# One stock of 19 tile buffers for loads and outputs, and later stores, in a chunked RWKV-WKV kernel

## The chip, the cores and the metric

The kernel runs on one core of a Trainium2 chip. TensorE (PE) multiplies matrices into PSUM, VectorE (DVE) and ScalarE (ACT) do elementwise work, GpSimd (POOL) does small work, and SyncE (SP) only issues transfers between HBM and SBUF. The transfers are carried by 16 DMA engines. The metric is the device time of one execution in microseconds (us). Profile times are counted from the start of the span, which runs from the first to the last instruction.

## The reference

The inputs are `k` and `v` of shape (16, 2048, 256) in float32 (batch, time, channel), and `w` and `u` with one number for each channel. For every batch and channel there is a recurrence over time with a numerator state `aa`, a denominator state `bb` and a running maximum `pp` that keeps the exponentials in range:

```python
ww = u + kk; qq = np.maximum(pp, ww)
e1, e2 = np.exp(pp - qq), np.exp(ww - qq)
output[b, t, :] = (e1 * aa + e2 * vv) / (e1 * bb + e2 + 1e-08)
ww = pp - w + kk; qq = np.maximum(ww, kk)      # qq becomes the next pp
e1, e2 = np.exp(ww - qq), np.exp(kk - qq)
aa = e1 * aa + e2 * vv
bb = e1 * bb + e2
```

So an output is a ratio of two decayed sums over all earlier steps, in which the current step counts with the bonus `u`. Without intermediate results, 67.1 MB are read and 33.5 MB are written.

## The kernel before

**Tiles.** Time is cut into 16 chunks of 128 steps, and a chunk into four tiles of four batches each, so there are NP = 64 tiles. Tile n belongs to chunk n // 4. It has its 128 steps on the partitions and 4 x 256 = 1024 columns (batch, channel). Each tile needs one load of `k`, one load of `v` and one store, each of 512 KB and each one DMA. That makes 191 large DMAs, and four of 128 KB for the last tile.

**The work of one tile.** `round_k` (DVE, L176) copies the loaded keys to a type that PE takes, and with that the load's buffer is free again. `logs` (PE) adds decay terms to the keys in PSUM, and `exps` (ACT, L204) takes the exponential of both variants (without and with the bonus) into the ring `EZR` of 12 tiles. `cast_v` (DVE, L209) copies the loaded values to bf16, which frees the other buffer, and `times_v` (DVE, L214) multiplies. `den` (PE) sums the denominators over time. `den_log` (ACT, L346) takes their logarithm out of PSUM into a buffer `RD[n]`, and `den_exp` (ACT, L349) turns it there into the reciprocal. `num` (PE, L358) sums the numerators, and `mult` (DVE, L362), in two halves, multiplies them into the same buffer. `store` (SP, L365) sends that buffer to HBM. Between chunks, small steps (`sums`, `turn`, `state_...`, `turn_back`, `inject`) carry the state on. They need several slots, which is why outputs run LAG = 10 tiles behind the exponentials.

**Slots.** The order on every engine is the order in which the program text emits the instructions. Slot n is one pass of a loop: `exps(n)`, then the rounding of the keys of tile n+2, the casting of values, `times_v(n)` and `logs(n+1)`. From slot 10 on it also has `den` and the reciprocal of tile n-10, and the two `mult`s of tile n-11. In a slot, ACT has `exps(n)`, then `den_log(n-10)`, then `den_exp(n-10)`. After slot 63 a tail works off the remaining outputs, of which ACT's two exponentials of the very last tile are done by halves.

**Transfers.** All loads and stores are issued by SP from one queue, in program order. In `before` they have three pools of fixed size: six buffers for keys, five for values, and eight for outputs. At the start of slot n, `load(n + AHEAD)` emits the loads of the values of tile n+5 and the keys of tile n+6. Then `store(qp - 2)` follows, which is the output of tile n-13:

```python
load(n + AHEAD)
if qp >= 2:            # qp = n - 11
    store(qp - 2)
```

A load waits on SP until the buffer that it takes has been rounded or cast. `den_log` of tile q takes the output buffer of tile q-8, and waits on ACT until that tile's store has landed. A transfer also waits for the eighth transfer before it, whose semaphore it takes over.

Of the kernel before, what the change touches and what calls it, by code (L numbers as in the profile page):

```python
# [7 lines left out]
F32 = mybir.dt.float32  # L8
# [7 lines left out]
def kernel(  # L16
# [9 lines left out]
    K = tc.keep_in_program_order  # L26
    PE, DVE, SC, POOL, SP = nc.tensor, nc.vector, nc.scalar, nc.gpsimd, nc.sync

    B, T, Dm = k.shape
# [3 lines left out]
    D = 2 * Dm  # L33
    NP = 4 * NST
    RING = 12
    AHEAD = 6
    LAG = 10
    RS = 2.0 ** -20
    CAP = 54.0
    ON_DVE = (0, 1, NST - 1)  # L40

    consts = ctx.enter_context(tc.tile_pool(name="consts", bufs=1))
    kpool = ctx.enter_context(tc.tile_pool(name="kpool", bufs=AHEAD))
    vpool = ctx.enter_context(tc.tile_pool(name="vpool", bufs=5))
    vbpool = ctx.enter_context(tc.tile_pool(name="vbpool", bufs=4))
    rpool = ctx.enter_context(tc.tile_pool(name="rpool", bufs=8))
    small = ctx.enter_context(tc.tile_pool(name="small", bufs=2))
    tiny = ctx.enter_context(tc.tile_pool(name="tiny", bufs=1))
    ps = ctx.enter_context(tc.tile_pool(name="ps", bufs=1, space=bass.MemoryType.PSUM))
# [2 lines left out]
    kr_of, vr_of, VB = {}, {}, {}  # L52

    def rows_of(x, n):
        c, p = divmod(n, 4)
        return x[4 * p:4 * p + 4, c * TC:(c + 1) * TC, :].rearrange("n t d -> t n d")

    def load_k(n, queue=SP):
        kr_of[n] = kpool.tile([128, 4, Dm], F32, tag="kr", name="kr")
        K(queue.dma_start(out=kr_of[n], in_=rows_of(k, n)))  # L60

    def load_v(n, queue=SP):
        vr_of[n] = vpool.tile([128, 4, Dm], F32, tag="vr", name="vr")
        K(queue.dma_start(out=vr_of[n], in_=rows_of(v, n)))


    def load(n):
        if n - 1 < NP:
            load_v(n - 1)
        if n < NP:  # L70
            load_k(n)

    def matrix(name, dt):
        return consts.tile([128, 128], dt, tag=name, name=name)

    def fill(ap, value):
        K(DVE.memset(ap.bitcast(F32) if ap.dtype == F32R else ap, value))
# [27 lines left out]
    load_k(1)  # L107
    load_row(SP, 1, 2, u)
    load_v(0)
    for n in range(2, AHEAD):  # L110
        load_k(n)
        load_v(n - 1)
    K(SC.preload_act_table_set("natural_log_exp_and_others"))
# [34 lines left out]
    def out_matrices(*names):  # L148
        if "L" in names:
            for h in range(2):  # L150
                fill(Lx[HS * h:HS * h + HS, HS * (1 - h):HS * (2 - h)], 0.0)
        for name in names:
            x, f = I1 if name[0] == "I" else Lx, RS if name[-1] == "N" else 1.0
            mats[name] = matrix(name, BF16)
            K(DVE.tensor_single_scalar(mats[name], x, f, op=ALU.mult))
# [15 lines left out]
    def ez(n):  # L171
        return EZR[:, :, n % RING]

    def round_k(n):
        km = consts.tile([128, 4, Dm], F32R, tag=f"km{n % 2}", name="km") if n < 2 else KM[n - 2]
        K(DVE.tensor_copy(km, kr_of.pop(n)))  # L176
        KM[n] = km

    def logs(n):
        km = KM[n].rearrange("p (i n) d -> p i (n d)", i=2)  # L180

        def rows(q):
            for i in range(2):
                g = 32 * (2 * q + i)
                K(PE.matmul(half(n, q)[:, i, :], CO[g:g + 32, :],  # L185
                            WU[g:g + 32, :].unsqueeze(1).broadcast_to([32, 2, Dm]), start=True, stop=False,
                            tile_position=(g, 0), skip_group_check=True))

        def steps(q):
            for i in range(2):  # L190
                K(PE.matmul(half(n, q)[:, i, :], (NLE, NLZ)[q], km[:, i, :], start=False, stop=True,  # L191
                            skip_group_check=True))

        rows(0)
        rows(1)
        steps(0)
        steps(1)

    def exps(n):
        if n < TURNS:  # L200
            for q in range(2):
                K(SC.activation(ez(n)[:, q], half(n, q), ACT.Exp))  # L202
        else:
            K(SC.activation(ez(n)[:, 0:2], PS[:, 0:4, :].rearrange("p (q i) x -> p q i x", q=2), ACT.Exp))  # L204

    def cast_v(n):
        vb = vbpool.tile([128, 4, Dm], BF16, tag="vb", name="vb")
        vr = vr_of.pop(n)
        K(DVE.tensor_copy(vb, vr))  # L209
        VB[n] = vb  # L210

    def times_v(n):
        vb = VB.pop(n).rearrange("p (i n) d -> p i (n d)", i=2)
        K(DVE.tensor_mul(ez(n)[:, 2:4], ez(n)[:, 0:2], vb.unsqueeze(1).broadcast_to([128, 2, 2, D])))  # L214
# [16 lines left out]
    def sums(n):  # L231
        c, p = divmod(n, 4)
        t = MISC[:, 0:Dm]
        for o in range(2):
            x = 24 - 16 * o - 2 * p
            for j in range(4):
                q, i = divmod(j, 2)
                K(PE.matmul(t[32 * j:32 * j + 32, :], mats["OH"][:, x:x + 32],  # L238
                            ez(n)[:, 2 * q, i, Dm * o:Dm * o + Dm],
                            start=p == 0 and o == 0, stop=p == 3 and o == 1,  # L240
                            tile_position=(0, 32 * j), skip_group_check=True))
# [94 lines left out]
    RD = {}  # L336
# [5 lines left out]
                            skip_group_check=True))  # L342

    def den_log(n, bank=DENB):
        RD[n] = rpool.tile([128, 2, D], F32, tag="rd", name="rd")
        K(SC.activation(RD[n], bank, ACT.Ln, scale=RS))  # L346

    def den_exp(n, i=slice(0, 2)):
        K(SC.activation(RD[n][:, i, :], RD[n][:, i, :], ACT.Exp, scale=-1.0))  # L349
# [10 lines left out]
    def mult(n, bank, i):  # L360
        rd = RD[n]
        K(DVE.tensor_mul(rd[:, i, :], bank, rd[:, i, :]))  # L362

    def store(n):
        K(SP.dma_start(out=rows_of(out, n), in_=RD.pop(n).rearrange("p i (n d) -> p (i n) d", n=2)))  # L365

    later = {}
    for c in range(NST):
# [19 lines left out]
    def small_work(n, where):  # L388
        for f, c in later.pop((n, where), []):
            f(c)  # L390

    def idle_matmuls(n, bank):
        for _ in range(n):
            K(PE.matmul(bank, idle[:, 0:128], idle, start=True, stop=True, skip_group_check=True))
# [5 lines left out]
    K(DVE.scalar_tensor_tensor(WU, WUH, Rest, wuf, ALU.mult, ALU.add))  # L400
    logs(0)
    round_k(1)
    cast_v(0)
    for n in range(LAG):

        load(n + AHEAD)
        exps(n)
        if n % 4 == 0 and n:
            sums(n - 1)
        small_work(n, "act")  # L410
        small_work(n, "logs")
        logs(n + 1)
        if n % 4:
            sums(n - 1)
        small_work(n, "pe")
        idle_matmuls(2, NUMB)
        times_v(n)
        small_work(n, "chain")
        round_k(n + 2)
        small_work(n, "round")  # L420
        cast_v(n + 1)
        if n < 4:
            (state_start, lambda: out_matrices("L"), lambda: out_matrices("IdN", "LN"),
             lambda: out_matrices("Id"))[n]()

    def inverses(n):
        q, qp = n - LAG, n - LAG - 1
        if qp >= 0:
            num(qp, NUMB, 1)

        sums(n - 1)
        if n + 1 < NP:
            recip(q, lambda: small_work(n, "recip"))

    for n in range(LAG, NP):

        q, qp = n - LAG, n - LAG - 1
        load(n + AHEAD)

        if qp >= 2:  # L440
            store(qp - 2)
        if qp >= 0:
            num(qp, NUMB, 0)
        den(q)
        small_work(n, "nums")
        exps(n)
        small_work(n, "act")
        if qp >= 0:
            mult(qp, NUMB, 0)
        small_work(n, "mid")  # L450
        if n == LAG:

            inverses(n)
            small_work(n, "early")
        if n + 2 < NP:
            round_k(n + 2)

        if n % 4 in (3, 0):
            cast_v(n)
        if n + 1 == NP:  # L460
            times_v(n)
        elif n % 4 < 2:
            cast_v(n + 1)
        if n > LAG:
            inverses(n)
        if qp >= 0:
            mult(qp, NUMB, 1)
        small_work(n, "scan")
        if n + 1 < NP:
            times_v(n)  # L470
            small_work(n, "chain")
            logs(n + 1)
        small_work(n, "pe")
# [4 lines left out]
    q, c = NP - LAG - 1, NST - 1  # L478
# [4 lines left out]
    def outputs(n):  # L483
        for i in range(2):
            mult(n, nbank(n, i), i)
        store(n)

    den_log(q)
    den(q + 1, dbank(q + 1))
    sums(NP - 1)  # L490
    copy_sums(c)
    store(q - 2)
    store(q - 1)
    den_exp(q)
    den_log(q + 1, dbank(q + 1))
    tile_num(q, 0)
# [9 lines left out]
    state_offsets(c)  # L506
    state_weights(c)
    mult(q, nbank(q, 1), 1)
    store(q)
    state_chain(c)  # L510
    den(q + 3, dbank(q + 3))
    for i in range(2):
# [14 lines left out]
    n, p = NP - 1, (NP - 1) % 4  # L527
    for i in range(2):
        den_exp(n, slice(i, i + 1))
        mult(n, nbank(n, i), i)  # L530
        for j, eng in ((0, SP), (1, SC)):
            b = 4 * p + 2 * i + j
            K(eng.dma_start(out=out[b, c * TC:(c + 1) * TC, :], in_=RD[n][:, i, Dm * j:Dm * j + Dm]))
# [31 lines left out]
```

## Time and profile before

| what | value |
|---|---|
| time, median of 3 runs (lowest to highest) | 290.09 us (289.56 to 290.15) |
| the profiled execution | 289.65 us, with a span of 288.0 us |
| mean granted TensorE clock | 0.988 |
| busy share of the span: PE, DVE, ACT, POOL | 91%, 91%, 88%, 37% |
| bytes moved, mean rate | 101.54 MB, 353 GB/s |
| issue to landing, median: keys, values, outputs | 8.3, 8.3, 8.1 us |

Engines wait for each other through semaphores. "Busy" is the time in which an engine executes, and an SP row is the time that SP needs to issue a transfer, not the time of the transfer itself. A busy share over the whole span is a mean over stages: an engine with 91% can be full in one stage and starved in another, so the stages have to be looked at one by one. The DMA share is the mean busy share of the 16 DMA engines, and in full stages it shows a little over 1.

### The profile page before, as it was taken

The page shows a single profiled execution, that of the slowest core. Times are in us where ns is not written, and L with a number is a line of the kernel's source. Part 1 is how long each engine was busy: PE and PEld are TensorE (multiplying, and loading weights), DVE is VectorE, ACT ScalarE, POOL GpSimd, SP SyncE. Part 2 cuts the span into 40 slices and gives each one's busy share as a digit, 9 for nine tenths or more (in the row PEclk, how much of TensorE's full clock was granted, in tenths as well). Part 3 has the DMA queues.
Part 4 walks back from the last instruction along what each step waited for, and adds up shares of the span by engine and source line. Part 5 has one row for each costly group of instructions (what it writes and reads, how often), then busy time and mean ns, then how long its engine had stood idle before and what let it go on. Part 6 is the DMA issues. An engine that isn't in the chain of part 4 may idle for free. (4 is left out here: it accounts for less than half of the span.)

```text
span 288.0 us, 5023 instructions
## 1 busy us (share of the span) xinstructions
PE 261.4 (91%) x1694; PEld 119.4 (41%) x1694; DVE 262.3 (91%) x463; ACT 254.7 (88%) x252; POOL 105.2 (37%) x208
## 2 busy tenths in 40 slices
PE   5997897999999999999999999899998989998990
PEld 1443443544444544435444444344344444433430
DVE  4698999999999999999999999998999999988863
ACT  2675678999999999999999989999998999998891
POOL 7000523352534454543525364460434435233000
PEclk9799999999999999999999999999999999999997
DMA  6999999999999999999999999999999999994697
GB/s 214 353 348 350 349 331 349 331 361 375 381 369 381 372 379 378 381 379 381 378 376 381 369 381 375 377 376 371 373 374 380 374 377 380 373 383 160 201 339 245
DMA packets 103587, 101.54 MB, mean 353 GB/s; under 512 B 4285, under 2 KB 103561, under 8 KB 103561
## 3 DMA queue, kind: packets, MB, share of 16 engines
q1 hardware_dynamic: 101336, 100.45, 102.6%
q0 software_dynamic: 1920, 0.50, 0.8%
q8 instruction: 13, 0.21, 0.3%
q10 hardware_dynamic: 304, 0.27, 0.3%
q14 instruction: 14, 0.11, 0.1%
HBM read 67.12 MB, written 33.55 MB: 350 GB/s over the span
## 5 line engine op out<-in xcount | busy, mean ns | idle before, releaser
L204 ACT ACTIVATE EZR<-PS 128x2048 bf16<-128x2048 f32 x54 | 101.2, 1875 | 7.5 <-PE PS L191 6.5
L362 DVE TENSOR_TENSOR rd<-PS,rd 128x512 f32<-128x512 f32 x128 | 87.0, 687 | 6.1 <-ACT rd L349 4.7
L214 DVE TENSOR_TENSOR EZR<-EZR,vb 128x2048 bf16<-128x2048 bf16 x64 | 78.1, 1220 | 2.2 <-ACT EZR L202 1.5
L349 ACT ACTIVATE rd<-rd 128x1024 f32<-128x1024 f32 (+1 forms) x65 | 67.9, 1047 | 2.7 <-DVE rd L362 1.8
L346 ACT ACTIVATE rd<-PS 128x1024 f32<-128x1024 f32 x64 | 65.7, 1026 | 0.8 <-PE PS L341 0.8
L358 PE MATMUL PS<-EZR,LN 128*128 128x512 bf16 x128 | 48.7, 381 | 12.2 <-DVE rd L362 8.4
L331 POOL DMA_DIRECT2D EZR<-cb x60 | 36.5, 614 | 52.1 <-DVE cb L326 45.4
L176 DVE CAST km<-kr 128x1024 fp32r<-128x1024 f32 x64 | 44.7, 699 | 6.9 <-DMA kr<-in_k_dram 6.4
L191 PE MATMUL PS<-km,NLE 128*128 128x512 f32 x128 | 47.5, 453 | 2.3 <-DVE km L176 2.2
L358 PE MATMUL PS<-EZR,IdN 128*128 128x512 bf16 x128 | 48.4, 378 | 0.0
L209 DVE CAST vb<-vr 128x1024 bf16<-128x1024 f32 x64 | 43.4, 694 | 0.7 <-DMA vr<-in_v_dram 0.7
L191 PE MATMUL PS<-km,NLZ 128*128 128x512 f32 x128 | 40.6, 398 | 0.0
L341 PE MATMUL PS<-EZR,Id 128*128 128x512 bf16 x128 | 38.1, 379 | 0.0
L341 PE MATMUL PS<-EZR,L 128*128 128x512 bf16 x128 | 38.1, 379 | 0.0
L185 PE MATMUL PS<-WU,CO 32*128 32x512 bf16 x256 | 27.2, 388 | 3.4 <-DVE WU L400 2.2
L269 POOL TENSOR_TENSOR F<-LL,LL 128x32 f32<-128x32 f32 x13 | 6.7, 515 | 61.9 <-ACT LL L260 61.9
L191 PEld LDWEIGHTS PS<-km,NLZ 128*128 128x128 f32 x128 | 24.4, 191 | 5.8
L191 PEld LDWEIGHTS PS<-km,NLE 128*128 128x128 f32 x128 | 19.3, 190 | 17.3 <-issue 12.9
L238 PE MATMUL PS<-EZR,OH 128*32 128x256 bf16 x512 | 26.1, 278 | 0.1
L202 ACT ACTIVATE EZR<-PS 128x1024 bf16<-128x1024 f32 x20 | 19.4, 1019 | 7.6 <-PE PS L191 7.6
L358 PEld LDWEIGHTS <-IdN 128*128 128x128 bf16 x128 | 12.5, 97 | 28.7 <-issue 26.3
L282 POOL TENSOR_TENSOR Q<-P,F 128x64 f32<-128x64 f32 x13 | 15.7, 1205 | 15.0 <-DVE P L273 15.0
(71 smaller groups left out, 200.0 us busy)
## 6 DMA issues: line engine op xcount, KB each, us to landing
kr<-in_k_dram SPq DMA_DIRECT2D x64, 512.0 KB, 8.3
vr<-in_v_dram SPq DMA_DIRECT2D x64, 512.0 KB, 8.3
out_dram<-rd SPq DMA_DIRECT2D x63, 512.0 KB, 8.1
EZR<-cb POOLq DMA_DIRECT2D x60, 8.0 KB, 5.3
out_dram<-rd SPq DMA_DIRECT2D x2, 128.0 KB, 2.7
out_dram<-rd ACTq DMA_DIRECT2D x2, 128.0 KB, 2.2
EZR<-cb SPq DMA_DIRECT2D x4, 8.0 KB, 1.9
wuf<-in_w_dram ACTq DMA_DIRECT2D x1, 8.0 KB
```

The costliest lines, as they stand in the source:

```text
L176: K(DVE.tensor_copy(km, kr_of.pop(n)))
L185: K(PE.matmul(half(n, q)[:, i, :], CO[g:g + 32, :], WU[g:g + 32, :].unsqueeze(1).broadcast_to([32, 2, Dm]), start=True, stop=False, tile_p ...
L191: K(PE.matmul(half(n, q)[:, i, :], (NLE, NLZ)[q], km[:, i, :], start=False, stop=True, skip_group_check=True))
L204: K(SC.activation(ez(n)[:, 0:2], PS[:, 0:4, :].rearrange("p (q i) x -> p q i x", q=2), ACT.Exp))
L209: K(DVE.tensor_copy(vb, vr))
L214: K(DVE.tensor_mul(ez(n)[:, 2:4], ez(n)[:, 0:2], vb.unsqueeze(1).broadcast_to([128, 2, 2, D])))
L331: K(queue.dma_start(out=EZR[r:r + 1, 2 * q, r0:r0 + 4, :, :].rearrange("o p i (b x) -> o (p i b) x", b=4), in_=cb[x:x + 32, :]))
L341: K(PE.matmul(bank[:, i, :], mats[m], ez(n)[:, q, i, :], start=q == 0, stop=q == 1, skip_group_check=True))
L346: K(SC.activation(RD[n], bank, ACT.Ln, scale=RS))
L349: K(SC.activation(RD[n][:, i, :], RD[n][:, i, :], ACT.Exp, scale=-1.0))
L358: K(PE.matmul(bank, mats[m], ez(n)[:, q, i, :], start=q == 2, stop=q == 3, skip_group_check=True))
L362: K(DVE.tensor_mul(rd[:, i, :], bank, rd[:, i, :]))
```

## The change

The three pools become one list of 19 buffers of equal size. Eight of them begin as output buffers (`free_out`) and eleven as load buffers (`free`). A load takes whichever load buffer became free first, for keys or values alike. Every list entry carries the slot from which it may be taken.

- **Loads** are emitted in the middle of a slot, behind `round_k` and `cast_v`, in pairs (`v` of one tile, `k` of the next) as long as two buffers are free. Counted through, that gives `v` of tile n+6 and `k` of tile n+7 at the end of slot n in the early slots.
- **Stores** are emitted behind the loads of the slot, and later: from slot 14 on, and then one slot later still at each of the slots 24, 30, 36, 42, 48 and 54. Once the last load is emitted, in slot 60, everything finished is stored.
- **An output buffer** may be taken again three slots after its store was emitted (`STORED`).
- **Handing over.** When fewer than three output buffers would be ready two slots ahead, one load buffer becomes an output buffer for good. That happens in slots 31, 37, 43, 49 and 55, so that the loads end with six buffers and the outputs with thirteen.
- **At the very end**, both halves of the last tile's `den_exp` are emitted ahead of both halves of `mult` and of the last four DMAs. Before, the second `den_exp` came behind the first half's DMA on ACT's queue.

The instructions of PE, DVE, ACT and POOL are the same in number, kind and order, but for that last pair on ACT.

```diff
-    AHEAD = 6
+    BUFS, OUTS = 19, 8
+    STORED = 3
...
+    bufs = [consts.tile([128, 4, Dm], F32, tag=f"buf{j}", name="buf") for j in range(BUFS)]
+    free = [(0, x) for x in bufs[OUTS:]]
+    free_out = [(0, x) for x in bufs[:OUTS]]
...
+    def loads(slot):
+        nonlocal loaded
+        if slot + 2 >= LAG and sum(x <= slot + 2 for x, _ in free_out) < 3:
+            free_out.append((slot + 2, take(slot, free)))
+        while loaded < NP and loaded - slot < 9 and sum(x <= slot for x, _ in free) >= 2:
+            load_v(loaded, slot)
+            loaded += 1
+            if loaded < NP:
+                load_k(loaded, slot)
...
     def den_log(n, bank=DENB):
-        RD[n] = rpool.tile([128, 2, D], F32, tag="rd", name="rd")
+        RD[n] = take(n + LAG, free_out).rearrange("p (i n) d -> p i (n d)", i=2)
...
-        load(n + AHEAD)
-
-        if qp >= 2:
-            store(qp - 2)
...
+        loads(n)
+
+        while stored < (qp - 2 - max(0, n - 18) // 6 if loaded < NP else qp):
+            store(stored, n)
+            stored += 1
...
     for i in range(2):
         den_exp(n, slice(i, i + 1))
+    for i in range(2):
         mult(n, nbank(n, i), i)
```

More of the change, by code (lines that the diff above doesn't have):

```diff
@@ L42 @@
     consts = ctx.enter_context(tc.tile_pool(name="consts", bufs=1))
-    kpool = ctx.enter_context(tc.tile_pool(name="kpool", bufs=AHEAD))
-    vpool = ctx.enter_context(tc.tile_pool(name="vpool", bufs=5))
     vbpool = ctx.enter_context(tc.tile_pool(name="vbpool", bufs=4))
-    rpool = ctx.enter_context(tc.tile_pool(name="rpool", bufs=8))
     small = ctx.enter_context(tc.tile_pool(name="small", bufs=2))
@@ L56, in rows_of, with take, load_k, load_v @@
         return x[4 * p:4 * p + 4, c * TC:(c + 1) * TC, :].rearrange("n t d -> t n d")
[L58 to L71, printed above, removed]
+    bufs = [consts.tile([128, 4, Dm], F32, tag=f"buf{j}", name="buf") for j in range(BUFS)]
+    free = [(0, x) for x in bufs[OUTS:]]
+    free_out = [(0, x) for x in bufs[:OUTS]]
+    def take(slot, of):
+        j = min(range(len(of)), key=lambda j: of[j][0])
+        assert of[j][0] <= slot
+        return of.pop(j)[1]
+    def load_k(n, slot=0):
+        kr_of[n] = take(slot, free)
+        K(SP.dma_start(out=kr_of[n], in_=rows_of(k, n)))
+    def load_v(n, slot=0):
+        vr_of[n] = take(slot, free)
+        K(SP.dma_start(out=vr_of[n], in_=rows_of(v, n)))
+    loaded = 5
+    def loads(slot):
[7 more added lines that the diff above has]
+                load_k(loaded, slot)
     def matrix(name, dt):
@@ L109 @@
     load_v(0)
-    for n in range(2, AHEAD):
+    for n in range(2, 6):
         load_k(n)
@@ L172, in ez, with round_k @@
         return EZR[:, :, n % RING]
-    def round_k(n):
+    def round_k(n, slot=0):
         km = consts.tile([128, 4, Dm], F32R, tag=f"km{n % 2}", name="km") if n < 2 else KM[n - 2]
-        K(DVE.tensor_copy(km, kr_of.pop(n)))
+        kr = kr_of.pop(n)
+        K(DVE.tensor_copy(km, kr))
+        free.append((slot, kr))
         KM[n] = km
@@ L204, in exps, with cast_v @@
             K(SC.activation(ez(n)[:, 0:2], PS[:, 0:4, :].rearrange("p (q i) x -> p q i x", q=2), ACT.Exp))
-    def cast_v(n):
+    def cast_v(n, slot=0):
         vb = vbpool.tile([128, 4, Dm], BF16, tag="vb", name="vb")
@@ L209, in cast_v @@
         K(DVE.tensor_copy(vb, vr))
+        free.append((slot, vr))
         VB[n] = vb
@@ L362, in mult, with store @@
         K(DVE.tensor_mul(rd[:, i, :], bank, rd[:, i, :]))
-    def store(n):
-        K(SP.dma_start(out=rows_of(out, n), in_=RD.pop(n).rearrange("p i (n d) -> p (i n) d", n=2)))
+    def store(n, slot):
+        rd = RD.pop(n).rearrange("p i (n d) -> p (i n) d", n=2)
+        K(SP.dma_start(out=rows_of(out, n), in_=rd))
+        free_out.append((slot + STORED, rd))
     later = {}
@@ L418 @@
         small_work(n, "chain")
-        round_k(n + 2)
+        round_k(n + 2, n)
         small_work(n, "round")
-        cast_v(n + 1)
+        cast_v(n + 1, n)
+        loads(n)
         if n < 4:
@@ L424 @@
              lambda: out_matrices("Id"))[n]()
+    stored = 0
     def inverses(n):
@@ L437 @@
         q, qp = n - LAG, n - LAG - 1
-        load(n + AHEAD)
-        if qp >= 2:
-            store(qp - 2)
         if qp >= 0:
@@ L455 @@
         if n + 2 < NP:
-            round_k(n + 2)
+            round_k(n + 2, n)
         if n % 4 in (3, 0):
-            cast_v(n)
+            cast_v(n, n)
         if n + 1 == NP:
@@ L462 @@
         elif n % 4 < 2:
-            cast_v(n + 1)
+            cast_v(n + 1, n)
+        loads(n)
+        while stored < (qp - 2 - max(0, n - 18) // 6 if loaded < NP else qp):
+            store(stored, n)
+            stored += 1
         if n > LAG:
@@ L485, in outputs @@
             mult(n, nbank(n, i), i)
-        store(n)
+        store(n, n + LAG)
     den_log(q)
@@ L491 @@
     copy_sums(c)
-    store(q - 2)
-    store(q - 1)
+    for n in range(stored, q):
+        store(n, q + LAG)
     den_exp(q)
@@ L508 @@
     mult(q, nbank(q, 1), 1)
-    store(q)
+    store(q, q + LAG)
     state_chain(c)
```

## The prediction

> **What bounds the kernel now.** I read the stages first, because the mean busy shares of the page mix different limits. This table by stretches has, behind the stretch, its length, then the busy time of PE, weight loads, DVE, ACT and POOL, the clock, the DMA share and GB/s:
>
> ```profile
> 60.00:160.00 100.00, 97.80 (x656) 45.04 (x655) 99.05 (x165) 98.77 (x94) 44.69 (x83) 1.00 1.09 377
> 160.00:250.00 90.00, 83.28 (x550) 38.21 (x549) 84.40 (x137) 84.23 (x81) 36.28 (x66) 1.00 1.09 375
> 250.00:268.00 18.00, 16.43 (x108) 7.07 (x107) 15.83 (x37) 15.84 (x18) 6.15 (x13) 1.00 0.80 279
> 268.00:280.00 12.00, 11.57 (x54) 5.12 (x53) 8.86 (x14) 12.00 (x14) 0.00 (x0) 1.00 0.83 272
> ```
>
> From 60 to 160, PE, DVE and ACT are all 98 to 99% busy and the DMA engines are full too (1.09). From 160 to 250 the DMA engines are still full, but the others have dropped to 93 or 94%. After 250 the DMA has room. So two limits lie close together, and the slightly slower one, DMA, takes over at 160. The list of waits for 160 to 250 names it (total us, times, longest):
>
> ```profile
> DVE km L176 <- DMA kr<-in_k_dram: 4.9, 14, 0.6
> ```
>
> For 60 to 160 that list has no DVE or ACT wait. Next, the pace, by the starts of `exps` (L204) in ACT's timeline: slots 20, 40, 41 and 63.
>
> ```profile
> 79.58 1.88 ACT L204 ACTIVATE EZR<-PS 128x2048 bf16<-128x2048 f32 x1
> ...
> 159.04 1.88 ACT L204 ACTIVATE EZR<-PS 128x2048 bf16<-128x2048 f32 x1
> ...
> 162.93 1.89 ACT L204 ACTIVATE EZR<-PS 128x2048 bf16<-128x2048 f32 x1
> ...
> 256.77 1.88 ACT L204 ACTIVATE EZR<-PS 128x2048 bf16<-128x2048 f32 x1
> ```
>
> Unstarved: (159.04 - 79.58) / 20 = 3.973 us a slot. Starved: (256.77 - 162.93) / 22 = 4.265. What late keys cost is 22 x 0.292 = 6.4 us. Last, SP's queue, with the issues of keys 13 and 19 and of stores 10, 12, 16 and 17:
>
> ```profile
> 36.29 1.55 SPq L60 DMA_DIRECT2D kr<-in_k_dram  x1
> ...
> 55.12 1.42 SPq L60 DMA_DIRECT2D kr<-in_k_dram  x1
> ...
> 99.71 1.34 SPq L365 DMA_DIRECT2D out_dram<-rd  x1
> ...
> 108.12 1.25 SPq L365 DMA_DIRECT2D out_dram<-rd  x1
> ...
> 124.57 1.30 SPq L365 DMA_DIRECT2D out_dram<-rd  x1
> ...
> 128.94 1.28 SPq L365 DMA_DIRECT2D out_dram<-rd  x1
> ```
>
> Loads alone go at (55.12 - 36.29) / 12 = 1.57 us each. Two loads and a store take (128.94 - 99.71) / 7 = 4.18, more than the 3.973 of a slot. In this mix a store adds 4.18 - 2 x 1.57 = 1.04 at least, or a third of the trio, 1.39.
>
> **What the skill says.** The Trainium skill, "DMA: Bandwidth & Descriptors", section "Queues, rings and completion order", says that each DMA engine takes the descriptors of a ring in order. The trace agrees: keys, values and outputs have the same 8.3, 8.3 and 8.1 us from issue to landing, so a transfer waits for those ahead. Its section "Anatomy of one DMA — SWDGE (gpsimd) path" says that waiting for a semaphore happens on the issuing sequencer, not in the DMA engines. So one blocked entry of SP's queue holds back all behind it. "Perfetto Trace Analysis", "Optimization Strategy" under "Identifying Performance Opportunities", advises interleaving regimes in which different engines are contended. That fits the table: DMA has room after 250, and stores could go there.
>
> **The change, part by part.**
>
> *Fewer stores ahead of the loads (gain).* Before, the last keys (tile 63) stand behind 44 stores, in the new order behind 39. The five stores are worth 5 x 1.04 = 5.2 to 5 x 1.39 = 7.0 us. Needed are 6.4 for full pace up to slot 63. On the way the lead is three to five stores from slot 38 on, while the deficit grows by 0.29 a slot, so it covers it. Taken: up to 6.4, at least 5.2.
>
> *A new wait on ACT (loss).* `den_log` of tile q writes into a buffer whose old output must have landed. Before, that is tile q-8, whose store was emitted five slots earlier. Now store 10 is emitted in slot 25, and `den_log(18)` takes its buffer in slot 28. How late is that store? Count the large transfers up to and including it. Before, store m is number 3m + 40 (keys to m+19, values to m+18, m+1 stores). Now stores 10 to 15 are number 3m + 46 (keys to m+22, values to m+21). So new store m takes the place of old store m+2. The DMA engines are full from the start, so the place sets the time. Store 12 was issued at 108.12 and lands at about 108.12 + 8.1 = 116.2. But ACT comes to `den_log` of slots 28 and 32 at
>
> ```profile
> 113.14 1.02 ACT L346 ACTIVATE rd<-PS 128x1024 f32<-128x1024 f32 x1
> ...
> 129.04 1.02 ACT L346 ACTIVATE rd<-PS 128x1024 f32<-128x1024 f32 x1
> ```
>
> In slot 28, ACT stands for 116.2 - 113.14 = 3.1 us. Slots 29 to 32 take buffers with the same three slots in between, at 4.18 of DMA for 3.97 of work. By slot 32 (store 14 in the place of store 16: 124.57 + 8.1 = 132.7) the delay is 132.7 - 129.04 = 3.6. Besides, the first 88 transfers now hold two more loads and two fewer stores, 2 x (1.57 - 1.04) = 1.1 if a store in the mix is that cheap, else 0. I take 0.55, so 4.2, with ends 3.6 and 4.7. Behind the waiting `den_log` are `den_exp(18)`, `exps(29)` and all else of ACT, for which `mult`, `times_v` and then PE wait. ACT and DVE are 99% busy here, so none of it is made good.
> From slot 33 it ends: tile 23 takes a handed-over buffer, so store 15 (slot 30) has four slots until slot 34. ACT's delay meanwhile lets the DMA run ahead.
>
> *Six load buffers instead of eleven (late slots).* By then compute is 4.2 late, so a key load has that reserve over the DMA place. A buffer freed in slot 59 is used in slot 61, 7.9 us later, against 8.3 with a full queue. But loads that wait for buffers keep the queue short. Taken at 0, bound 0 to 4 us (see the rivals).
>
> *SP, in the order of the queue.* A load now stands behind `round_k` and `cast_v` of its own slot. Up to slot 28 SP is further behind than that (keys 31, emitted in slot 25 at 99, were issued at 106.80), so nothing is added. No engine's work changes; the number and bytes of transfers are equal, so 0.
>
> *The stores left over.* 24 stores instead of 19 follow the last values. At 1.4 us, the 13 up to store 52 take 18 us from about 248, so they land by 267. Stores from 54 on become ready at ACT's pace (1.85 us in the tail), after 267, so the tail stays ACT's: it is 12.00 of 12 busy from 268 to 280. The four small DMAs of `inject` are queued behind some stores, but are read only some 4 us later (`den(60)`, 273). So 0, bound 0 to 1.
>
> *Both last exponentials together.* Before, the second sits behind the first half's DMA:
>
> ```profile
> 280.46 1.89 DVE L362 TENSOR_TENSOR rd<-PS,rd 128x512 f32<-128x512 f32 x3 [0.57 <-ACT rd L349]
> ...
> 282.38 0.36 ACTq L533 DMA_DIRECT2D out_dram<-rd  x1
> 282.80 0.63 ACT L349 ACTIVATE rd<-rd 128x512 f32<-128x512 f32 x1 [1.84 <-DVE rd L362]
> 283.46 0.69 DVE L362 TENSOR_TENSOR rd<-PS,rd 128x512 f32<-128x512 f32 x1 [1.11 <-ACT rd L349]
> ```
>
> The last `mult` can now follow at 282.4, which is 1.1 earlier. But the last pair of DMAs is then issued 0.7 behind the pair ahead, whose 256 KB take 0.7 themselves and stand behind store 62 (issued 281.8, some 3 us to land). I take 0.1 gain; ends 0 and 1.1.
>
> *Sum.* 6.4 - 4.2 + 0.1 = 2.3 us of the 288.0 span. That span's run took 289.65, 0.4 below the median. I set the same 2.3 against the median: 290.09 - 2.3 = **287.8**.
>
> **The rivals.**
> *B, no wait.* Store 10 lands before 113.1, or the wait is taken up elsewhere. For: before it is emitted, no store is added in slot 24. Against: the count of places, with the DMA full. Then 290.09 - 6.4 - 0.1 = 283.6; with half the wait 285.7.
> *C, the wait goes on (slower).* Place: `den_log` on ACT from slot 33 on. If stores with three slots keep landing late, each slot costs 4.18 - 3.97 = 0.21. Over 31 slots that is 6.5: 287.8 + 6.5 = 294.3. It decides from 2.9 us more (change 0.2% slower), which is 0.09 a slot. For: most stores keep just three slots. Against: five buffers are handed over, and from slot 37 on fewer than three transfers a slot are asked for.
> *D, keys late again from too few buffers.* If issue to landing stays at 8.3 with six buffers (from slot 56 on) or seven (from 50), the old pace returns for up to 14 slots: 14 x 0.29 = 4.1, so 291.9. Against: the queue is then shorter.
>
> **How the numbers follow.** No change would be measured within 0.2%, that is 0.58 us: 289.5 to 290.7. My forecast has 0.60 (own range 286.3 to 289.4, from the ends of wait and stores), B 0.18, C 0.12, D 0.10. All of the forecast but 0.03 and all of B are faster, and a brief D or C of 0.04: 0.79. Of C and D, 0.06 end within the bound with that 0.03: 0.09. The rest, 0.12, is slower. The range 284.0 to 290.3 leaves out B's better third and the slower part.
>
> **What would show it.** In the new profile: no DVE wait of note for key loads in 160 to 250; a new wait of ACT's `den_log` on store transfers, of 3 to 4 us at slot 28 (about 113 us) and small ones to slot 32, then none; slots of 3.97 after that; `exps(63)` at about 254.6; DMA full to about 115, then less so; a fuller DMA after 250. Wrong would make it: no such wait, waits after 135, or key waits that persist.

## The result, and the profile after

| | before | after |
|---|---|---|
| time, median of 4 runs each (lowest to highest) | 290.08 us (289.56 to 290.15) | 288.36 us (288.11 to 288.79) |
| span of the profiled execution | 288.0 us | 286.8 us |
| start of `exps(28)` | 111.36 us | 111.66 us |
| start of `exps(63)` | 256.77 us | 253.60 us |
| from the start of `exps(63)` to the end of the span | 31.2 us | 33.2 us |

The ratio is 0.9946, with a 95% interval of 0.9929 to 0.9963. So the changed kernel is 1.7 us faster, 0.6 us short of the forecast. The last three rows tell more than the sum does: up to `exps(63)` 3.2 us were gained, and the tail behind it gave 2.0 back.

In the changed kernel the lines have other numbers: `round_k` is L193, `exps` L222, `inject` L350, `den` L360, `den_log` L365, `den_exp` L368, `mult` L381, `store` L385, and the four last transfers L558. All buffers are now called `buf`.

The stages of the kernel after, in the same columns as before (stretch, length, busy time of PE, weight loads, DVE, ACT, POOL, clock, DMA share, GB/s):

```profile
60.00:160.00 100.00, 95.00 (x635) 43.73 (x633) 96.44 (x162) 96.16 (x92) 40.70 (x78) 1.00 1.09 377
160.00:250.00 90.00, 88.09 (x593) 40.80 (x592) 89.24 (x147) 89.04 (x87) 39.63 (x74) 1.00 1.06 360
250.00:268.00 18.00, 16.09 (x99) 6.93 (x98) 14.63 (x35) 15.78 (x18) 4.58 (x11) 1.00 1.03 354
268.00:280.00 12.00, 10.48 (x46) 4.19 (x44) 8.79 (x15) 11.08 (x13) 0.00 (x0) 1.00 0.91 299
```

From 160 to 250, DVE and ACT are now 99% busy (89.24 and 89.04 of 90) where before they had 84. The DMA engines are no longer what binds there. From 60 to 160 ACT lost 2.6 us: that is the new wait. After 250 the DMA is fuller than before (1.03 against 0.80), and ACT, which was busy for all of the 12.00 us from 268 to 280, is now busy for 11.08: it works without a gap and has done its last instruction at 279.08.

The new wait stands in ACT's timeline of slot 28: `exps(28)`, and then `den_log(18)` with the idle time ahead of it in brackets. Below them is SP's issue of store 10, the output whose buffer it takes.

```profile
111.66 1.88 ACT L222 ACTIVATE EZR<-PS 128x2048 bf16<-128x2048 f32 x1
116.15 1.02 ACT L365 ACTIVATE buf<-PS 128x1024 f32<-128x1024 f32 x1 [2.61 <-DMA out_dram<-buf]
```

```profile
107.59 1.23 SPq L385 DMA_DIRECT2D out_dram<-buf  x1
```

Store 10 lands at 116.06, 8.5 us after its issue, and ACT goes on 0.1 us later. The list of waits for 111 to 135 (total us, times, longest) has it all:

```profile
ACT buf L365 <- DMA out_dram<-buf: 2.8, 2, 2.6
```

The whole execution has the same 2.8, so nothing of it comes after 135. The wait for late keys, 4.9 us from 160 to 250 before, has no line in that stretch any more. The pace from slot 41 to slot 63 is read from

```profile
166.18 1.89 ACT L222 ACTIVATE EZR<-PS 128x2048 bf16<-128x2048 f32 x1
...
253.60 1.88 ACT L222 ACTIVATE EZR<-PS 128x2048 bf16<-128x2048 f32 x1
```

(253.60 - 166.18) / 22 = 3.974 us a slot: the unstarved pace.

In the tail two waits are new. The first is at the last but one chunk's injection: `den(56)` on PE needs rows that four small DMAs of POOL bring into `EZR`, and ACT's `den_log` waits for PE. From the timelines of PE and ACT:

```profile
261.91 0.59 PE L360 MATMUL PS<-EZR,L 128*128 128x512 bf16 x2 [1.65 <-DMA EZR<-cb]
262.97 1.02 ACT L365 ACTIVATE buf<-PS 128x1024 f32<-128x1024 f32 x1 [1.57 <-PE PS L360]
```

The second is in SP's queue. Before it stood so (start, time for all the issues of the row):

```profile
266.77 2.52 SPq L331 DMA_DIRECT2D EZR<-cb  x4
269.39 12.80 SPq L365 DMA_DIRECT2D out_dram<-rd  x9
```

and after:

```profile
264.38 3.95 SPq L350 DMA_DIRECT2D EZR<-cb  x4
268.43 11.37 SPq L385 DMA_DIRECT2D out_dram<-buf  x9
279.99 2.42 SPq L558 DMA_DIRECT2D out_dram<-buf  x2
```

The last chunk's four small DMAs of 8 KB begin 2.4 us earlier than before, but SP takes 3.95 us to issue them in place of 2.52. So the nine stores from 54 on begin only 0.96 us earlier. From then on they are in arrears: stores 54 to 61 land 1.55 us apart on average, and store 62 lands 4.95 us after its issue, where before it took 3.06. Before, ACT set the end; now a backlog of stores does. The time around those four DMAs, in the windows of after:

```profile
265.00:270.00 5.00, 4.89 (x24) 2.06 (x23) 4.16 (x7) 5.00 (x6) 0.00 (x0) 1.00 0.58 184
270.00:280.00 10.00, 8.59 (x38) 3.48 (x36) 7.23 (x13) 9.08 (x11) 0.00 (x0) 1.00 1.03 340
```

From 265 to 270 the DMA engines are only half used (0.58), while finished outputs stand behind the small DMAs on SP; from 270 on they are full.

### The profile page after: what moved, and what is told of

It is laid out like the page before. It is cut to its first block, busy times and chain, and to the rows that moved or that the text cites. A ratio compares the mean times of both kernels' runs of the same rounds, so it can differ in the third digit from the quotient of the medians.

```text
span 286.8 us, 5076 instructions
## 1 busy us (share of the span) xinstructions
PE 261.9 (91%) x1694; PEld 119.5 (42%) x1694; DVE 261.0 (91%) x463; ACT 254.0 (89%) x252; POOL 104.3 (36%) x208
## 4 chain that ended last, share of the span: by engine, by line
DVE 38%; PE 21%; DMA 16%; ACT 12%; issue 10%; DVEq 1%; POOL 0%; ACTq 0%; POOLq 0%
DVE EZR L233 15%; DVE buf L381 11%; PE PS L209 8%; PE PS L377 7%; DMA buf<-in_k_dram 6%; DMA out_dram<-buf 6%; ACT buf L368 4%; DVE km L193 4%; ACT buf L365 4%; DVE vb L227 3%; PE PS L203 3%; PE PS L257 3%; ACT EZR L222 2%; DMA EZR<-cb 2%; DMA wuf<-in_u_dram 2%
## 5 line engine op out<-in xcount | busy, mean ns | idle before, releaser
L222 ACT ACTIVATE EZR<-PS 128x2048 bf16<-128x2048 f32 x54 | 101.2, 1875 | 3.6 <-PE PS L209 2.6
L381 DVE TENSOR_TENSOR buf<-PS,buf 128x512 f32<-128x512 f32 x128 | 86.9, 687 | 8.0 <-ACT buf L368 3.6
L365 ACT ACTIVATE buf<-PS 128x1024 f32<-128x1024 f32 x64 | 65.9, 1029 | 4.6 <-DMA out_dram<-buf 2.8
L368 ACT ACTIVATE buf<-buf 128x1024 f32<-128x1024 f32 (+1 forms) x65 | 67.8, 1048 | 0.9
L350 POOL DMA_DIRECT2D EZR<-cb x60 | 36.8, 619 | 53.2 <-DVE cb L345 46.5
L193 DVE CAST km<-buf 128x1024 fp32r<-128x1024 f32 x64 | 43.9, 686 | 1.4 <-DMA buf<-in_k_dram 1.3
L227 DVE CAST vb<-buf 128x1024 bf16<-128x1024 f32 x64 | 43.2, 691 | 0.3 <-DMA buf<-in_v_dram 0.3
L360 PE MATMUL PS<-EZR,L 128*128 128x512 bf16 x128 | 38.1, 379 | 1.8 <-DMA EZR<-cb 1.6
L360 PE MATMUL PS<-EZR,Id 128*128 128x512 bf16 x128 | 38.1, 379 | 0.0
L288 POOL TENSOR_TENSOR F<-LL,LL 128x32 f32<-128x32 f32 x13 | 8.2, 631 | 65.5 <-ACT LL L279 65.5
L377 PEld LDWEIGHTS <-LN 128*128 128x128 bf16 x128 | 12.8, 100 | 18.4 <-issue 11.3
```

The source lines that it names most:

```text
L193: K(DVE.tensor_copy(km, kr))
L350: K(queue.dma_start(out=EZR[r:r + 1, 2 * q, r0:r0 + 4, :, :].rearrange("o p i (b x) -> o (p i b) x", b=4), in_=cb[x:x + 32, :]))
L360: K(PE.matmul(bank[:, i, :], mats[m], ez(n)[:, q, i, :], start=q == 0, stop=q == 1, skip_group_check=True))
L377: K(PE.matmul(bank, mats[m], ez(n)[:, q, i, :], start=q == 2, stop=q == 3, skip_group_check=True))
```

## The experiments

The theories after this reading. *Wait and tail*: the change costs 2.8 us in slot 28, and the tail gives back 2.0 since a backlog of stores meets `inject` on SP. *The DMA engines are the bound throughout*: they have a fixed amount to carry, so a wait that is taken away returns elsewhere. Each number below is a median with its lowest and highest, and the ratio, with its 95% interval, is that to the kernel before measured beside it (289.75 us for the first four experiments, 290.05 for the next four, 289.89 for the last). Since the kernel before itself differs by 0.3 us between these sets, a difference to the kernel after's 288.36 is no surer than that.

**The wait in slot 28 taken away.** An output buffer may be taken again four slots after its store, not three. The rule for handing over then gives six load buffers away, the first in slot 26.

```diff
-    STORED = 3
+    STORED = 4
```

> The changed kernel with STORED = 4: an output buffer is taken again four slots after its store was emitted, not three, and a load buffer is handed over already in slot 26 (six in all). Theory 1 (the end is set by the DMA engines: they are full from the start to about 266, and then drain the last ten stores at 1.54 us each): ACT's wait of 2.6 us on a store in slot 28 goes, exps(63) moves from 253.6 to 251 to 252 (then the keys limit), but store 54 is issued at about 268 as before, so the time stays within 0.4 us of the changed kernel's 288.4. Theory 2 (the end is set by ACT's chain behind exps(63)): the 2 to 3 us come through to the end, about 286.

Measured: 287.37 us (286.63 to 287.65), ratio 0.9911 (0.9879 to 0.9943). That lies between the two theories. ACT has no wait on a store any more and `exps(63)` starts at 252.12, but now one key is late. From DVE's timeline, `round_k(63)` in slot 61:

```profile
245.78 0.69 DVE L193 CAST km<-buf 128x1024 fp32r<-128x1024 f32 x1 [1.12 <-DMA buf<-in_k_dram]
```

From `exps(28)` (111.94) to `exps(63)` there are 140.18 us, 1.76 less than after; the other 1.12 of the wait of 2.8 came back as that late key, and 1.0 us reached the median. So both theories are wrong in part. The DMA engines do not set a fixed end, because from 205 to 250 they are not full:

```profile
205.00:250.00 45.00, 41.78 (x280) 19.80 (x284) 43.22 (x70) 44.15 (x43) 19.43 (x37) 1.00 1.06 354
```

The kernel before carried 376 GB/s in this stretch (share 1.09), the kernel after 355. A reason lies in the rule. Every six slots it withholds one store and gives away one load buffer, so of 18 transfers it asks for 16. Those are 16 x 0.524 MB in 6 x 3.974 us, or 352 GB/s. SP's own waits fit this: in the kernel after, from 200 to 250, the loads of keys (L69) and of values (L73) stand on SP until `round_k` (L193) has freed a buffer for them, and all that is queued behind them stands as well (total us, times, longest).

```profile
SPq L69 <- DVE km L193: 8.6, 4, 2.7
SPq L73 <- DVE km L193: 7.3, 3, 3.4
```

The kernel before has no such wait in that stretch. What is not carried then is carried in the tail.

The late key of this run has the same root. Six hand-overs leave the loads with five buffers. The load of key 63 was issued at 238.11, right after this `cast_v` had freed the buffer that it takes, and it landed at 245.76:

```profile
237.39 0.69 DVE L227 CAST vb<-buf 128x1024 bf16<-128x1024 f32 x1
```

**The last chunk's injection on POOL.** The four small DMAs leave SP's queue, and the stores behind them needn't wait for their issue.

```diff
-    inject(c, SP)
+    inject(c)
```

> The changed kernel with the last chunk's four small state DMAs (inject) issued by POOL instead of SP, so that store 54 no longer stands behind them on SP. Theory 1 (the tail is drained by the DMA engines): the hole in the DMA share between 265 and 270 (0.58) closes, store 54 is issued at about 266 instead of 268.4, and the end comes 1.2 to 1.6 us earlier, about 287.0. Theory 2 (ACT's chain sets the end): no change, within 0.4 us of 288.4.

Measured: 287.0 us (286.9 to 287.42), ratio 0.9905 (0.9877 to 0.9933), 1.4 less than after by the medians, 1.2 by the ratios. The wait of slot 28 is still there (2.4 us with a small second one). The window of the tail now reads

```profile
265.00:270.00 5.00, 4.25 (x19) 1.78 (x19) 4.17 (x8) 5.00 (x7) 2.00 (x4) 1.00 1.01 331
```

The DMA engines are full (1.01 against 0.58), store 54 is issued at 265.71 in place of 268.43, and store 62 lands 2.99 us after its issue: the end is ACT's again. The edit has a small price: the last chunk's rows now land 4.3 to 4.7 us after their issue, and PE waits 0.7 us for them. How much of the lost 2.0 us was due to the backlog, the next run tells.

**The same edit on the kernel before**, to see whether it is worth anything without a backlog.

```diff
-    inject(c, SP)
+    inject(c)
```

> The kernel before with the same edit (inject of the last chunk on POOL). Before, store 62 lands 3.1 us after its issue, so the backlog has melted and ACT sets the end. Theory 1: within 0.4 us of 290.1. If the four DMAs on SP cost as much in the kernel before as in the changed one, about 288.7.

Measured: 289.25 us (288.65 to 290.21), ratio 0.998 (0.9965 to 0.9995), a gain of 0.2% or 0.6 us. That is a little more than the 0.4 that the first theory allowed, and less than half of what the edit brings to the kernel after. So of the 1.4 us, some 0.8 came with the backlog, and 0.6 can be had without one. The profiled executions, split where SP issues store 62, say the same (us):

| | before | before, `inject` on POOL | after | after, `inject` on POOL |
|---|---|---|---|---|
| from `exps(63)` to the issue of store 62 | 25.05 | 25.06 | 25.83 | 26.04 |
| from there to the end of the span | 6.1 | 5.6 | 7.3 | 5.7 |

The second row is the price of the backlog: 1.2 us from before to after, and nearly nothing with `inject` on POOL. The first row is the chain of work on ACT. It lost 0.8 us, and `inject` on POOL does not give that back. The two make up the 2.0.

**Stores evenly late.** The step by one slot in every six is taken out, so that store m is emitted in slot m+14 all the way. Buffers, pairs of loads and hand-over rule stay, and no buffer is then handed over.

```diff
-        while stored < (qp - 2 - max(0, n - 18) // 6 if loaded < NP else qp):
+        while stored < (qp - 2 if loaded < NP else qp):
```

> The changed kernel with stores that stay three slots late all the way (no further slot every six): the last keys stand behind 42 stores (44 before, 39 in the changed kernel), nothing is handed over, output buffers have four slots between store and reuse. Theory 1: no ACT wait of 2.6 us, small ones instead, exps(63) at about 254.4, and since the DMA engines have the same total to carry, the time is that of the changed kernel within 0.5 us. Theory 2 (each store taken from ahead of the keys counts): three stores more ahead, 3.6 us later keys, less the 2.6 us wait: about 289.4.

Measured: 288.77 us (288.38 to 289.22), ratio 0.9962 (0.995 to 0.9973). That is 0.4 above after, with intervals that overlap: what the withheld stores bring over this simpler rule is little, on balance. ACT's waits on stores are spread over the late slots. From the waits of 160 to 250:

```profile
ACT buf L365 <- DMA out_dram<-buf: 2.4, 9, 0.5
```

The 35 slots from `exps(28)` to `exps(63)` take 143.35 us in its profile, 1.4 more than after. The tail makes up for that: from `exps(63)` it has 30.7 us, 2.5 less than after. It has a free DMA, which is seen from 255 to 265:

```profile
255.00:260.00 5.00, 4.65 (x35) 1.88 (x34) 4.83 (x10) 4.97 (x7) 1.94 (x4) 1.00 0.64 220
260.00:265.00 5.00, 4.39 (x26) 1.91 (x20) 4.29 (x16) 4.48 (x7) 0.76 (x3) 1.00 0.35 115
```

Here the DMAs of the last but one injection land 1.7 to 2.0 us after their issue, and PE does not wait for them. In the kernel after, the same DMAs take 5.4 to 5.6 us in a full DMA (1.09 from 255 to 260), and PE waits.

**The last exponentials together, alone on the kernel before.**

```diff
     for i in range(2):
         den_exp(n, slice(i, i + 1))
+    for i in range(2):
         mult(n, nbank(n, i), i)
```

> The kernel before with the last edit alone: both halves of the last den_exp ahead of the last mults and DMAs. Prediction's price: the last pair of DMAs is issued 1.1 us earlier (0.7 us behind the pair ahead), but lands only 0.1 earlier, so 290.0. If the issue counts and not the queue, 1.1 us less, 288.9.

Measured: 289.96 us (289.15 to 291.54), ratio 0.9994 (0.9977 to 1.0011). No effect that can be measured. The forecast took 0.1 us for it, which is too small to be seen in an interval of 0.5 us to either side; a gain of 1.1 us, its other end, is ruled out.

**Both repairs together**, to see whether the wait and the tail add up or hide each other.

```diff
-    STORED = 3
+    STORED = 4
...
-    inject(c, SP)
+    inject(c)
```

> The changed kernel with both edits: STORED = 4 (no ACT wait in slot 28, worth 1.0 alone) and the last inject on POOL (worth 1.2 to 1.4 alone). Theory 1a (two separate losses: stores held and loads waiting for buffers leave the DMA engines short of work in slots 37 to 60, and the last inject on SP holds store 54 back): they add up, 286.0. Theory 1b (only the total of DMA work sets the end, so the second edit finds nothing left): 287.0.

Measured: 285.45 us (285.11 to 286.42), ratio 0.9843 (0.9803 to 0.9883). Against after, 1.0 and 1.4 alone, 2.9 together: within an interval of 1.2 us to either side they add up, so the two are separate costs. The DMA still carries 355 GB/s from 205 to 250, with 0.8 us of late key in slot 61.

**One buffer more.** A 20th buffer for outputs, with its space taken from the ring of cast values.

```diff
-    BUFS, OUTS = 19, 8
+    BUFS, OUTS = 20, 9
...
-    vbpool = ctx.enter_context(tc.tile_pool(name="vbpool", bufs=4))
+    vbpool = ctx.enter_context(tc.tile_pool(name="vbpool", bufs=3))
```

> The changed kernel with one buffer more (BUFS, OUTS = 20, 9; its room is taken from the cast values, three instead of four), so that output buffers keep four slots up to slot 33 and the loads end with seven buffers instead of six. Theory 1a: ACT's wait in slot 28 goes, and the DMA share in slots 45 to 60 (1.05 in the changed kernel) rises, so the end comes at least as early as with STORED = 4: 286.8 to 287.4. If load buffers don't matter there, 287.4 and an unchanged share; if the wait only moves to slot 34, up to 288.4.

Measured: 287.86 us (287.21 to 288.09), ratio 0.9921 (0.989 to 0.9952). The wait has not gone, it has moved to slot 34. From ACT's timeline, `exps(34)` and `den_log(24)`:

```profile
135.53 1.88 ACT L222 ACTIVATE EZR<-PS 128x2048 bf16<-128x2048 f32 x1
139.57 1.02 ACT L365 ACTIVATE buf<-PS 128x1024 f32<-128x1024 f32 x1 [2.16 <-DMA out_dram<-buf]
```

From 205 to 250 the DMA carries 356 GB/s, as in the kernel after (355), though seven load buffers are left at the end and not six. So one buffer more does not raise the rate, while the rule still asks for 16 transfers in six slots. It also shows where the wait comes: counted through, slot 34 is here the first in which only three slots lie between a store's emission and the next use of its buffer, as slot 28 is in the kernel after. Nearly all later slots of both kernels have three as well, but wait little (0.2 us in all after, 0.6 here).

**Everything together**: 20 buffers (with the ring of cast values at three, as above), `STORED = 4` and `inject` on POOL.

```diff
-    BUFS, OUTS = 19, 8
-    STORED = 3
+    BUFS, OUTS = 20, 9
+    STORED = 4
...
-    inject(c, SP)
+    inject(c)
```

> All three edits on the changed kernel: 20 buffers, STORED = 4, last inject on POOL. Theory 1a: at or below the two edits without the extra buffer, 285.3 to 286.0. Theory 1b: 287.0.

Measured: 286.25 us (286.1 to 287.23), ratio 0.9872 (0.9833 to 0.9911). Not better than the kernel with both repairs; the intervals overlap, so a cost of the 20th buffer is not shown either. The two profiled executions come to slot 28 at 113.52 and 111.74, which is further apart than the medians are, and why executions differ in their start the runs do not say. From `exps(28)` to `exps(63)` this one takes 138.99 us, the full pace, against 139.82 with both repairs: six load buffers are left here and not five, and no key is late.

**Steps of ten slots.** The two repairs, and the withholding done by one slot in every ten. By the reading of the first experiment the rule then asks for 28 transfers in ten slots: 28 x 0.524 MB in 39.7 us, or 370 GB/s.

```diff
-    STORED = 3
+    STORED = 4
...
-        while stored < (qp - 2 - max(0, n - 18) // 6 if loaded < NP else qp):
+        while stored < (qp - 2 - max(0, n - 18) // 10 if loaded < NP else qp):
...
-    inject(c, SP)
+    inject(c)
```

> The changed kernel with STORED = 4, the last inject on POOL, and a store one slot later only every ten slots, not every six (no other difference to the version with both edits, which took 285.5). Theory 1a says that in slots 32 to 55 the rule itself asks for 2.67 transfers a slot only (one store and, by the handed-over buffer, one load less in six slots), which is 353 GB/s at 3.97 us a slot, as measured (354 to 356 from 205 to 250), while the DMA engines could carry 375. With ten slots it is 2.8 transfers, 370 GB/s: the last keys are no longer late (0.8 us in slot 61), the backlog in the tail is smaller, 284.6 to 285.4. Rival: the last keys stand behind one store more (40 instead of 39), and the rate was limited by something else: the same 355 GB/s, and 286 or later.

Measured: **284.43 us** (284.25 to 284.95), ratio 0.9816 (0.9789 to 0.9843), the fastest of all. From 205 to 250:

```profile
205.00:250.00 45.00, 43.97 (x301) 20.14 (x298) 44.01 (x73) 44.43 (x43) 20.49 (x39) 1.00 1.09 380
```

DVE and ACT stay at the full pace (44.01 and 44.43 of 45), and the DMA is full again, with 380 GB/s. That is more than the 370 worked out, so the count of transfers gives the direction and not the exact rate. A queue that has still to be worked off may be the reason: in the kernel after, in steps of six slots from slot 32 on, the rates are 378, 374, 360, 353 and 358 GB/s, so that the rule's 352 was only reached after some 70 us. Nor does the run tell the rate of asking from the stock of load buffers, since it gives away only three of them while there are loads and keeps eight. Four waits of ACT on stores, 1.3 us in all, lie ahead of 205. What remains in its tail is PE's wait for the last but one injection:

```profile
PE PS L360 <- DMA EZR<-cb: 1.4, 1, 1.4
```

No run took this wait away by itself. That it comes from the full DMA rests on the profile of the evenly late stores, where the DMA is free and the wait is absent.

## Why the prediction was right, and where it was not

The sign, and the time within the likeliest case's own range, came out; but the sum is right in part because two errors cancel. In the profiled spans the account is: 35 slots from `exps(28)` to `exps(63)` took 145.41 us before and 141.94 after, 3.47 less. At 3.973 a slot they would take 139.06. So before lost 6.35 to late keys, and after loses 2.88.

- *Fewer stores ahead of the loads, 6.4*: right. 6.35 were to be had, and no key is late from 160 to 250, with slots of 3.974. But fewer stores alone would not quite have done it: ACT's wait of 2.9 us helped the loads too, since the work came later. In the first experiment, with that wait gone, a key is 1.12 us late.
- *The new wait on ACT, 4.2*: right in place and cause, wrong in size. Its core, counting places in the queue, was within 0.15 us: forecast 116.2 for the landing of store 10, measured 116.06. Of the 3.1 us in slot 28, 2.61 came, as this execution was 0.3 us later at that point. The added terms failed: slots 29 to 32 were to add another 0.5, and two loads more in the queue 0.55, and only 0.18 came. The measured total, 2.8, lies below the low end of 3.6. The queue did not fall back any further once ACT stood still, which the prediction had granted only from slot 33. Its reason for that end was wrong, too: counted through, store 15 is emitted in slot 31 and not in 30, so slot 34 has three slots like those before it, and still no wait.
- *Six load buffers, 0*: right for the kernel as it is, and the experiments with seven and with five buffers differ little in their rate in that stretch (356 and 354 GB/s). Rival D did not come, but its cause is real: both runs with five buffers have a late key (1.12 and 0.8 us), and none of the other variants of the changed kernel, with six and more, has one. What the step did not see is that the rule as a whole asks for 16 transfers in six slots, where about 17 fit at 376 GB/s: from 205 to 250 the DMA ran at 355. Over 45 us these 21 GB/s are 0.95 MB, or almost two stores that went into the tail.
- *SP's order, 0*: no sign against it; from 60 on, no engine waits for a load.
- *The stores left over, 0, bound 0 to 1*: this is the step that failed. It cost 2.0 us, outside its bound. The working checked that the backlog up to store 52 would be gone by 267, and that `den(60)` reads the injected rows late enough. It did not ask what the four small DMAs do to the stores *behind* them on SP: in a full queue they take 3.95 us to issue, not 2.52, and stores 54 on start in arrears. That part is some 1.2 us by the split at store 62, or 0.8 by the medians (1.4 with the backlog, less 0.6 without). Nor did it ask about the injection of POOL before it, which lands later in a full DMA and holds up PE, and ACT for 1.57 us. Before, ACT had no such wait there, but waited 0.76 us for PE one output later, behind `turn_back`, which is gone now. So this share is some 0.8 us; no run isolated it.
- *Both last exponentials, 0.1*: not contradicted. Alone the edit makes 0.9994 (0.9977 to 1.0011), which rules out the upper end of 1.1 but cannot show 0.1.

Taken together: 6.35 - 2.88 = 3.47, less 0.30 for a later start, less 2.0 in the tail gives 1.2 for the spans, 288.0 to 286.8. The forecast had 6.4 - 4.2 + 0.1. A wait sized 1.3 too large and a tail sized 2.0 too small mostly cancel.

Of the rivals, B (no wait) fails on the 2.61 us in slot 28. C (the wait goes on) fails too, with no such wait after 135. The run with evenly late stores shows C's mechanism at a small size: 2.4 us in nine waits when no buffer is handed over, there with four slots from a store to its buffer's next use.

## What to carry to other kernels

When a change moves transfers out of a full stage into a later one, go through the later stage as if it were full: the issue of every small DMA in the same queue, and every engine that reads a small transfer in time only while the DMA is idle. A rule that holds back stores and trades away buffers also fixes how many transfers a slot may ask for; work out its rate in GB/s and compare it with what the DMA engines can carry, because what lies below it is paid for at the end. And a forecast that meets the time can hold two errors of opposite sign: it is the split by stages, here at `exps(63)`, that shows them.

## What the runs showed of the hardware

- Issuing four DMAs of 8 KB on SP took 2.52 us when few transfers were under way, and 3.95 us behind a backlog of stores of 512 KB (3.80 with `STORED = 4`, 3.08 with the 20th buffer).
- DMAs of 8 KB that POOL issues from a queue of its own landed 1.7 to 2.0 us after their issue when the DMA engines were at 0.35 to 0.64, and 5.4 to 5.6 us after it when they were full. A separate queue did not shield them.
- The rate of the full DMA engines was not the same for all transfers: 383 and 384 GB/s with stores alone from 250 to 260, 377 to 380 in the mix of two loads and a store, and 340 with stores alone from 270 to 280, where they also read as full (1.03). Why the last differs from the first was not tried.
